# A hybrid layer on one core: the last small product of a triangular inverse takes a turning bank, and the last attention head is scaled behind the split of the memory keys

## The chip, the cores and the metric

The kernel runs on one core of a Trainium2 chip. The time is that of one execution on the device in microseconds (us); less is better. The engines named below are TensorE (PE in the profile; PEld is its loading of weights), VectorE (DVE), ScalarE (ACT), GpSimd (POOL) and SyncE (SP, which issues most of the transfers). PSUM is the memory into which TensorE writes; the kernel uses it in eight banks of 128 partitions by 512 fp32 numbers.

## The reference, cut to what matters

One inference step of one layer for 512 prompt tokens and 64 sample tokens, D = 1024, all in fp32:

```python
h = x + concat(GDN(n), DiffAttn(n)) @ w_out          # n = rmsnorm(x), one projection n @ w_in feeds both
h = h + MemCrossAttn(rmsnorm(h), mk, mv)             # mk, mv = rmsnorm(mem) @ w_mem_k, @ w_mem_v
h = h + relu(rmsnorm(h) @ w_ff1) ** 2 @ w_ff2
y = rmsnorm(h)
```

Two pieces of it are touched. The gated delta group (GDN, 4 heads of 128) goes over the tokens in chunks; in each chunk it solves a unit lower triangular system and carries a state:

```python
a_sys = where(strict, b[:, None] * kk * gam, 0) + eye(C)      # kk = k k^T, gam = decay between tokens
u = triangular_solve(a_sys, b * v);  w = triangular_solve(a_sys, b * exp(G) * k)
vn = u - w @ S
o  = qg @ S + qk @ vn
S  = S * exp(G_last) + kd.T @ vn                              # kd = k * exp(G_last - G): the state product
```

The differential attention (4 heads of 128) ends each head with a norm over its 128 numbers: `ob = rmsnorm(ob, diff_norm) * (1 - lam_init)`, and the heads go through `w_out`. The keys and values of the memory (256 tokens) are projections of their own.

## The kernel before

Activations lie with the features on the partitions. A projection takes 128 columns of a weight at a time: the weight block is loaded (512 KB), ACT casts its high part (`wh`, L159), DVE subtracts it for the low part (`wl`, L160, 128x1024), and 40 matmuls (8 of 512 columns, 8 of 256, 24 of 320) sum high and low parts in a bank of the tag `pr`, which turns over three banks. All matmuls are recorded at L106/107 (`mm`), all transposes at L111/113 (`tr`), so tiles tell them apart.

The eight PSUM banks are dealt by tag: `pr` 3, `ba` 2, `g0`, `g1` and `gs` one each. The banks of a tag turn in the order in which the program asks for them: the third user of `ba` waits until the first user's readers are done. The same holds for the SBUF tiles with two buffers, `kd` among them. A scheduler lays down one fixed order of instructions for each engine, by due times and by these dependencies; on the chip each engine runs its list strictly from the top, so an instruction that waits holds up whatever stands behind it on that engine.

**GDN.** The prompt is cut into chunks 0 to 3 of 128 tokens; the sample's 64 tokens are chunk 4, with half as many products. Each chunk has a preparation and a scan. `gdn_prep` (L653) works on the bank `g0` or `g1` by the chunk's parity. It turns the keys (`each(tr, kb)`) and makes `kd` of them (L680, DVE) and their squares (L682 ACT, L683 DVE); turns the queries (L686, L687); makes the decay, `At` = the strict part of the system (L712), `KQ` (L716) and `vb` (L719). Then it inverts the triangular system by doubling: X = I - B and its transpose (L736, L737, L752, L753), and levels of block size 2, 4, 8, 16, 32 (the loop from L757). A level is two transposes and a small product on one bank, a copy of the one (ACT, L765) and a masked copy of the other (DVE, L766), a second product, and two subtractions (DVE, L773 and L774; the last level has only L774). After the last level four transposes give X (ACT copy L776). In chunks 0 to 3 the two halves of 64 are then joined: a small product `by` (from `At` and `Dt`, 64x64 for each head, L779 to L781), its copy (ACT, L782), a second small product with X (on g0/g1), and L786 writes the last block of X.

`gdn_scan` (L814) carries the state: products on the bank `gs` give `r` (L830), `vn` (L833) and the output, and the state product kd x vn, four products of 128x128, goes to a bank of the tag `ba` (L841); four DVE operations (L797) add it to S. The program asks for the work in the order: preparation of chunk 0; then for c = 0 to 3 the preparation of chunk c+1, and behind it the scan of chunk c. Within c = 0 there stand also `turn_memory` (L905), which turns the normed memory tokens over the `ba` banks, and the projection of z. The projections of the attention heads fill the gaps on TensorE.

**Attention heads.** `diff_project(h)` projects q, k and v of head h and turns k and v over `ba`; head 0's k is written to memory that the normed memory tokens of `turn_memory` held. `diff_head(h, between)` does the head: scores, softmax, values, and the sum of squares `so`. `factors()` (POOL, L1118 and L206) makes the norm's factors `co` from it. `finish()` (L1124) scales the head (`an` = `an` * `co`, DVE 128x640, L1127), turns it over `ba` and writes it for `w_out` with ACT (L1133). A head's `finish` runs within the next head, the last one's within the memory projections, where also the split of the turned memory keys stands (`split_turned`, DVE, L1154).

The names in rows of the order end in numbers: `g0_310`, `g1_328`, `ba_319` are the 310th, 328th and 319th tile asked for (a second number is the program's own).

Of the kernel before, what the change touches and what calls it, by code (L numbers as in the profile page):

```python
# [11 lines left out]
ALU = mybir.AluOpType  # L12
# [3 lines left out]
P = 128  # L16
# [8 lines left out]
H = 4  # L25
# [12 lines left out]
def hybrid_layer_kernel(  # L38
# [9 lines left out]
    nc = tc.nc  # L48
    V, A, G = nc.vector, nc.scalar, nc.gpsimd
# [29 lines left out]
    def nm(s):  # L79
        uid[0] += 1  # L80
        return f"{s}_{uid[0]}"

    def pair(slot, dt=F32):

        return up.tile([P, 2, 4, T], dt, tag=f"u{slot}", name=nm("u"))
# [6 lines left out]
    def small(tag, shape, bufs=None, dt=F32):  # L92
        tag = SHARED.get(tag, tag)
        bufs = 1 if tag in ("vn", "on", "S", "qz") or tag[:-1] in ("At", "Dt", "Y") else 2
        return sp.tile(shape, dt, tag=tag, name=nm(tag), bufs=bufs)

    def tiny(shape, tag="tiny", bufs=16):
        return tp.tile(shape, F32, tag=tag, name=nm(tag), bufs=bufs)

    def bank(tag="ba"):  # L100
        return ps.tile([P, 512], F32, tag=tag, name=nm(tag), bufs=BANKS[tag])
# [4 lines left out]
    def mm(out, lhsT, rhs, start=True, stop=True, pin=False, skip_group_check=False):  # L106
        i = nc.tensor.matmul(out, lhsT, rhs, start=start, stop=stop, skip_group_check=skip_group_check)  # L107
        if pin:
            tc.keep_in_program_order(i)

    def tr(out, in_, pin=False):  # L111
        n = in_.shape[0]
        i = nc.tensor.transpose(out, in_, ident[:n, :n])  # L113
        if pin:
            tc.keep_in_program_order(i)
# [37 lines left out]
    def split_weights(w, shape):  # L153
        raw = wp.tile(shape, F32, tag="raw", name=nm("raw"), bufs=3)
        nc.sync.dma_start(raw, w.rearrange("(k p) n -> p k n", p=P))
        wh = wp.tile(shape, F32R, tag="wh", name=nm("wh"))
        wl = wp.tile(shape, F32R, tag="wl", name=nm("wl"))
        with tc.high_priority():
            A.copy(wh, raw)  # L159
            V.tensor_tensor(wl, raw, wh.bitcast(F32), ALU.subtract)  # L160
        return wh, wl
# [43 lines left out]
    def rpow(out, in_, n=None):  # L205
        G.tensor_tensor(out, in_, bc(nhalf[: in_.shape[0], 0:1], list(in_.shape)), ALU.pow)  # L206
# [419 lines left out]
    def v4(ap, nb):  # L626
        return ap.rearrange("p (h n) -> p h n", h=4)[:, :nb, :]
# [25 lines left out]
    def gdn_prep(c, nb, L):  # L653
# [91 lines left out]
        def pairs(b, half, f):  # L745
            t = b[:, 256 * half : 256 * half + np_ * P].rearrange("p (i n) -> p i n", n=P)
            for i in range(np_):
                f(t[:, i, :], i)
            return t
# [7 lines left out]
        while lv <= last:  # L757
# [6 lines left out]
            by = pairs(b, 0, lambda o, i: mm(o, As[:, i, :], low[:, i * n : (i + 1) * n]))  # L764
# [11 lines left out]
        A.copy(X, each(tr, of(Dt)))  # L776
        if lv < size:
            G.memset(Y[:64, :, :64], 0.0)
            by = bank(f"g{c % 2}")  # L779
            for h in range(H):  # L780
                mm(by[64:, h * 64 : h * 64 + 64], At[:, h, 64:], Dt[:, h, :64])  # L781
            A.copy(Y[64:, :, :64], by[64:, :256].rearrange("p (h n) -> p h n", h=4))  # L782
            bx = bank(f"g{c % 2}")
            for h in range(H):
                mm(bx[:64, h * 64 : h * 64 + 64], Y[:, h, :64], X[:, h, 64:])
            V.tensor_scalar(  # L786
                X[:64, :, 64:], bx[:64, :256].rearrange("p (h n) -> p h n", h=4), -1.0, None, ALU.mult
            )
# [125 lines left out]
    S, behind = None, lambda: None  # L914
    prepared = [gdn_prep(*chunks[0])]
    for c, _, L in chunks[:4]:
# [5 lines left out]
        S, behind = gdn_scan(c, L, prepared[c], S)  # L922
# [152 lines left out]
    def diff_head(h, between):  # L1075


        hs = slice(h * P, (h + 1) * P)
        so, co = tiny([P, 5], "ta"), tiny([P, 5], "ta")
        on = small("an", [P, 5, P])  # L1080
        for t in (4, 0, 1, 2, 3):
            if t == 1:
                between()
            q0 = QT[t][0]
            nk = q0 + P if t < 4 else PAST + DEC
            nb = (nk + P - 1) // P
            if t == 4:
                sample_rows(h, hs, so, on)
                continue
            pr = {}  # L1090
            mx, l = tiny([P, 2], "ta"), tiny([P, 2], "ta")
            for c in (1, 0):
                b = bank(f"g{c}")
                for j in range(2):
                    mm(b[:, :nk], qs[h % 2][:, c, q0 : q0 + P], stacked[h][c][j][:, :nk], start=j == 0, stop=j == 1)
                V.memset(b[:64, nk - 64 : nk], -1e30)
                V.tensor_reduce(mx[:, c : c + 1], b[:, :nk], AX.X, ALU.max)
                V.tensor_scalar(mx[:, c : c + 1], mx[:, c : c + 1], -0.125, None, ALU.mult)
                p = small(f"p{c}", [P, 512])
                A.activation(p[:, :nk], b[:, :nk], AF.Exp, bias=mx[:, c : c + 1], scale=0.125, accum_out=l[:, c : c + 1])  # L1100
                pr[c] = p
            V.reciprocal(l, l)
            V.tensor_tensor(l[:, 1:2], l[:, 1:2], nlam, ALU.mult)
            V.tensor_scalar(pr[1][:, :nk], pr[1][:, :nk], l[:, 1:2], None, ALU.mult)
            V.scalar_tensor_tensor(pr[0][:, :nk], pr[0][:, :nk], l[:, 0:1], pr[1][:, :nk], ALU.mult, ALU.add)
            bt = bank()
            aT = small("aT", [P, 4, P])
            for kb in range(nb):
                tr(bt[:, kb * P : (kb + 1) * P], pr[0][:, kb * P : (kb + 1) * P])
            A.copy(aT[:, :nb, :], v4(bt, nb))  # L1110
            po = bank("gs")[:, :P]
            for kb in range(nb):
                mm(po, aT[:, kb, :], vtm[:, kb, hs], start=kb == 0, stop=kb == nb - 1)
            A.activation(pr[1][:, :P], po, AF.Square, accum_out=so[:, t : t + 1])
            A.copy(on[:, t, :], po)

        def factors():
            G.tensor_scalar(so, so, 1.0 / P, EPS, ALU.mult, ALU.add)  # L1118
            rpow(co, so)

        if h == H - 1:
            factors()

        def finish():  # L1124
            if h < H - 1:
                factors()
            V.tensor_tensor(on, on, co.unsqueeze(2).to_broadcast([P, 5, P]), ALU.mult)  # L1127
            b, b2 = bank(), bank()
            for t in range(4):
                tr(b[:, t * P : (t + 1) * P], on[:, t, :])  # L1130
            tr(b2[:, :P], on[:, 4, :])
            for src, ts_ in ((b, slice(0, SEQ)), (b2[:, DEC:P], slice(SEQ, T))):
                A.activation(od[:, h, ts_], src, AF.Identity, scale=dn)  # L1133

        return finish

    finish = lambda: None
    for h in range(H):
# [4 lines left out]
        finish = diff_head(h, finish)  # L1143
# [30 lines left out]
    for w, out in ((w_mem_k, o_mk), (w_mem_v, o_mv)):  # L1174
        dst = tokens
        for f in range(2):
            fs = slice(512 * f, 512 * f + 512)
            bs = [bank("pr") for _ in range(2)]
            for kc in range(4):
                wt = split_weights(w[0, 256 * kc : 256 * kc + 256, fs], [P, 2, 512])  # L1180
                if kc == 1:
                    turn_keys()
                    if out is o_mv and f == 0:
                        finish()
                for k in (2 * kc, 2 * kc + 1):
                    for t in range(2):
                        ts_ = slice(t * P, (t + 1) * P)
                        for j, (wi, x) in enumerate(((0, mh), (0, ml), (1, mh))):
                            mm(
                                bs[t], x[:, k, ts_], wt[wi][:, k % 2, :],  # L1190
                                start=(k == 0 and j == 0), stop=(k == KT - 1 and j == 2),
                            )
            for t in range(2):
                (A.copy if t else V.tensor_copy)(dst[:, t, fs], bs[t])
                if out is o_mv:
                    A.copy(mv[:, t, fs], dst[:, t, fs])
                    V.tensor_tensor(mvl[2 * t + f], dst[:, t, fs], mv[:, t, fs].bitcast(F32), ALU.subtract)
            nc.sync.dma_start(out[0, 0].rearrange("(b p) h d -> p b (h d)", p=P)[:, :, fs], dst[:, :, fs])
            turn_keys = key_turns(f, dst) if out is o_mk else lambda: None
            if out is o_mv and f == 0:  # L1200
                ob = pair(5, F32R)
                for h in range(H):
                    split_to((ob,), od[:, h, :], h, 0)
# [513 lines left out]
```

## Time and profile before

| what | value |
|---|---|
| median of 3 runs | 977.6 us (976.36 to 977.66) |
| profiled execution | 977.09 us, of which the span of the profile is 975.3 us |
| TensorE busy | 960.4 us, 98% of the span |
| VectorE / ScalarE / GpSimd busy | 689.4 / 536.9 / 66.6 us |
| HBM | 92 GB/s over the span |
| granted TensorE clock | 0.998 |

A row of the timeline gives the start in the span, the duration, engine, line, operation, tile written <- tiles read, and in square brackets the idle time before it with what ended it. A row of groups by source line gives the least, median and greatest duration in ns and from when to when the line ran. A row of windows gives a stretch of the span, its length, and the busy time (and count) of PE, PEld, DVE, ACT and POOL in it, the granted clock, the share of the DMA engines and GB/s. In rows of the trace the numbers of the tiles are left out, so `g` is a tile of g0 or g1.

### The profile page before, as it was taken

What the parts mean: (1) busy time and instruction counts of PE and PEld (TensorE: products, weight loads), DVE (VectorE), ACT (ScalarE), POOL (GpSimd) and SP (SyncE); (2) the same over time, 40 slices, a digit from 0 to 9 for tenths busy, and PEclk for the clock granted to TensorE, in tenths of its full rate; (3) what the DMA queues carried; (4) which work ended last, traced back from release to release, by engine and by line L of the source; (5) the groups of instructions that cost most, each with busy time, mean ns of one, the idle gap of its engine ahead of it and who ended that gap; (6) DMA issues with size and microseconds to landing.
All of it is one profiled execution on the core that took longest, in us unless ns stands there. A gap on an engine that the chain in (4) does not pass through costs nothing.

```text
span 975.3 us, 16991 instructions
## 1 busy us (share of the span) xinstructions
PE 960.4 (98%) x6399; PEld 889.9 (91%) x6399; DVE 689.4 (71%) x1508; ACT 536.9 (55%) x1218; POOL 66.6 (7%) x158
## 2 busy tenths in 40 slices
PE   9999999998999999999999999999999999999996
PEld 7999998997888878999999999999999999999996
DVE  6655777776867776666657888567867779978674
ACT  6664774533656765435445567665544444545444
POOL 4341020211010000000000000000000000000000
PEclk9999999999999999999999999999999999999999
DMA  7442332120744666341121423332323223322202
GB/s 209 117 138 77 95 125 66 46 64 23 187 122 122 219 182 196 87 130 44 45 65 44 141 69 96 90 88 88 87 81 87 87 87 87 87 87 87 66 23 97
DMA packets 124915, 96.01 MB, mean 98 GB/s; under 512 B 6204, under 2 KB 112846, under 8 KB 124322
## 3 DMA queue, kind: packets, MB, share of 16 engines
q1 hardware_dynamic: 124466, 94.28, 33.6%
q8 instruction: 50, 0.82, 0.4%
q10 hardware_dynamic: 368, 0.66, 0.2%
q14 instruction: 31, 0.25, 0.1%
HBM read 79.93 MB, written 9.75 MB: 92 GB/s over the span
## 4 chain that ended last, share of the span: by engine, by line
PE 58%; issue 2%; DVE 1%; ACT 1%; DMA 0%; POOLq 0%; POOL 0%; ACTq 0%; DVEq 0%; SPq 0%
PE pr L107 37%; PE ba L107 10%; PE g L107 6%; PE gs L107 4%; PE ba L113 1%; DMA raw<-in_w_ff_dram 0%; ACT u L1596 0%; ACT c L1504 0%; DVE u L1552 0%; DVE w2l L1458 0%; ACT c L1503 0%; DVE w L1357 0%; DVE wl L1357 0%; DVE wh L1357 0%; ACT wl L1356 0%
## 5 line engine op out<-in xcount | busy, mean ns | idle before, releaser
L107 PE MATMUL pr<-u,wh 128*128 128x320 f32 (+2 forms) x1240 | 325.9, 341 | 0.1
L107 PE MATMUL pr<-u,wl 128*128 128x256 f32 (+1 forms) x816 | 226.1, 301 | 0.0
L107 PEld LDWEIGHTS pr<-u,wh 128*128 128x128 f32 x1240 | 212.1, 189 | 15.2 <-ACT u L286 0.3
L107 PEld LDWEIGHTS pr<-u,wl 128*128 128x128 f32 x816 | 150.5, 189 | 2.5 <-DVE wl L387 0.2
L160 DVE TENSOR_TENSOR wl<-raw,wh 128x1024 fp32r<-128x1024 f32 x65 | 79.5, 1223 | 56.5 <-ACT wh L159 56.3
L159 ACT CAST wh<-raw 128x1024 fp32r<-128x1024 f32 x65 | 68.2, 1049 | 61.9 <-PE pr L107 46.6
L107 PE MATMUL pr<-u,w2h 128*128 128x320 f32 (+1 forms) x384 | 98.5, 341 | 0.0
L1457 ACT CAST w2h<-r 128x512 fp32r<-128x512 f32 x56 | 34.7, 620 | 87.6 <-PE pr L107 85.4
L107 PE MATMUL pr<-f,w2h 128*128 128x320 f32 (+1 forms) x288 | 74.5, 341 | 0.5 <-DVE u L1546 0.5
L107 PEld LDWEIGHTS pr<-u,w2h 128*128 128x128 f32 x384 | 65.0, 188 | 4.5 <-ACT u L1542 0.3
L107 PE MATMUL pr<-u,w2l 128*128 128x256 f32 (+1 forms) x256 | 65.2, 296 | 0.0
L1544 DVE TENSOR_TENSOR u<-u,pr 128x256 f32<-128x256 f32 x96 | 42.4, 450 | 17.1 <-PE pr L107 16.5
L206 POOL TENSOR_TENSOR tiny<-tiny,nhalf 128x1 f32<-128x1 f32 (+4 forms) x10 | 8.8, 879 | 651.3 <-DVE tiny L1610 514.1
L107 PE MATMUL ba<-u,wl 128*128 128x288 f32 x360 | 52.9, 296 | 0.0
L107 PEld LDWEIGHTS pr<-f,w2h 128*128 128x128 f32 x288 | 48.8, 188 | 4.5 <-issue 1.7
L107 PEld LDWEIGHTS ba<-u,wl 128*128 128x128 f32 x360 | 49.2, 188 | 0.6 <-ACT keep L1494 0.5
L107 PE MATMUL pr<-f,w2l 128*128 128x256 f32 (+1 forms) x192 | 48.9, 295 | 0.0
L107 PEld LDWEIGHTS pr<-u,w2l 128*128 128x128 f32 x256 | 47.0, 189 | 1.5
L1458 DVE TENSOR_TENSOR w2l<-r,w2h 128x512 fp32r<-128x512 f32 x56 | 38.5, 688 | 9.6 <-ACT w2h L1457 9.4
L107 PE MATMUL pr<-wh,u 128*128 128x512 f32 x128 | 41.6, 400 | 0.1
L1503 ACT ACTIVATE c<-c 128x288 f32<-128x288 f32 x48 | 20.6, 443 | 28.5 <-DVE c L1502 28.5
L107 PEld LDWEIGHTS pr<-f,w2l 128*128 128x128 f32 x192 | 35.2, 189 | 1.1
(552 smaller groups left out, 2024.8 us busy)
## 6 DMA issues: line engine op xcount, KB each, us to landing
raw<-in_w_ff_dram SPq DMA_DIRECT2D x36, 512.0 KB
raw<-in_w_in_dram SPq DMA_DIRECT2D x28, 512.0 KB
r<-in_w_ff_dram SPq DMA_DIRECT2D x56, 256.0 KB
raw<-in_w_mem_k_dram SPq DMA_DIRECT2D x8, 512.0 KB
raw<-in_w_mem_v_dram SPq DMA_DIRECT2D x8, 512.0 KB
raw<-in_w_out_dram SPq DMA_DIRECT2D x8, 512.0 KB
raw<-in_w_mem_q_dram SPq DMA_DIRECT2D x8, 512.0 KB
raw<-in_w_mem_o_dram SPq DMA_DIRECT2D x8, 512.0 KB
```

Source lines behind the costliest of these rows:

```text
L107: i = nc.tensor.matmul(out, lhsT, rhs, start=start, stop=stop, skip_group_check=skip_group_check)
L113: i = nc.tensor.transpose(out, in_, ident[:n, :n])
L159: A.copy(wh, raw)
L160: V.tensor_tensor(wl, raw, wh.bitcast(F32), ALU.subtract)
L206: G.tensor_tensor(out, in_, bc(nhalf[: in_.shape[0], 0:1], list(in_.shape)), ALU.pow)
L1457: A.copy(wh, src)
L1458: V.tensor_tensor(wl, src, wh.bitcast(F32), ALU.subtract)
L1503: A.activation(c, c, AF.Relu)
L1544: V.tensor_tensor(am, am, b, ALU.add)
```

## The change

Three edits:

1. In `gdn_prep` the last step's small product `by` takes a bank of the turning tag `ba` where it took the chunk's own bank g0/g1 (chunks 0 to 3).
2. `factors()` is called at the end of each head. Before, only the last head did that; the others called it at the beginning of `finish`.
3. The last head's `finish` is handed the last instruction recorded so far, which belongs to the split of the memory keys, and its scaling is held behind that instruction.

```diff
@@ gdn_prep
         if lv < size:
             G.memset(Y[:64, :, :64], 0.0)
-            by = bank(f"g{c % 2}")
+            by = bank()
             for h in range(H):
                 mm(by[64:, h * 64 : h * 64 + 64], At[:, h, 64:], Dt[:, h, :64])
             A.copy(Y[64:, :, :64], by[64:, :256].rearrange("p (h n) -> p h n", h=4))
@@ diff_head
-        if h == H - 1:
-            factors()
-
-        def finish():
-            if h < H - 1:
-                factors()
-            V.tensor_tensor(on, on, co.unsqueeze(2).to_broadcast([P, 5, P]), ALU.mult)
+        factors()
+
+        def finish(behind=None):
+            with tc.issue_after(behind) if behind is not None else ExitStack():
+                V.tensor_tensor(on, on, co.unsqueeze(2).to_broadcast([P, 5, P]), ALU.mult)
             b, b2 = bank(), bank()
@@ the memory projections
                     if out is o_mv and f == 0:
-                        finish()
+                        finish(nc.cur_bb.bb.instructions[-1])
```

The order of instructions that the scheduler lays down differs well beyond these lines. Three places follow.

**TensorE, from the state product of chunk 1's scan to the preparations of chunks 3 and 4.** `ba_319` is that state product, `g0_310` the last transposes of chunk 2's inverse and `g0_311` or `ba_311` the small product that is edited; `g1_328` is the second set of transposes of chunk 3's preparation; `g1_361`, `g1_362`/`ba_362` are the same of chunk 3's inverse, `ba_370` the state product of chunk 2's scan, and `g0_379` is the second set of transposes of chunk 4's preparation. Before:

```order
L107 MATMUL ba_319_2101<-vn_317_2090,kd_196_1456 128x128
L107 MATMUL pr_527_3020<-u_6_91,wh_525_3016 128x512
...
L107 MATMUL g0_303_2018<-Y0_291_1967,X_290_1966 128x128 x2
L113 MATMUL g1_328_2131<-ident_79,u_4_78 128x128 x4
...
L113 MATMUL g0_310_2052<-ident_79,Dt0_292_1968 128x128 x4
...
L113 MATMUL g0_379_2346<-ident_79,u_4_78 128x128 x2
...
L113 MATMUL g1_361_2269<-ident_79,Dt1_343_2185 128x128 x4
```

and now:

```order
L113 MATMUL g0_310_2052<-ident_79,Dt0_292_1968 128x128 x4
L107 MATMUL ba_311_2059<-Dt0_292_1968,At0_283_1941 64x64 x4
L107 MATMUL ba_319_2101<-vn_317_2090,kd_196_1456 128x128 x4
...
L113 MATMUL g1_328_2131<-ident_79,u_4_78 128x128 x4
...
L113 MATMUL g1_361_2269<-ident_79,Dt1_343_2185 128x128 x4
L107 MATMUL ba_362_2276<-Dt1_343_2185,At1_335_2160 64x64 x4
L107 MATMUL ba_370_2318<-vn_368_2307,kd_274_1907 128x128 x4
L107 MATMUL g1_363_2282<-X_341_2183,Y1_342_2184 64x64 x4
L113 MATMUL g0_379_2346<-ident_79,u_4_78 128x128 x2
L107 MATMUL g0_384_2362<-triu2_1096,gg2_1184 128x128 x2
```

The state product of chunk 1 stood in the second level of chunk 2's inverse and now stands behind the whole of it; the preparation of chunk 3, which began before chunk 2's last levels, now begins after them, and that of chunk 4, which began amid chunk 3's levels, after those. Between `g1_328` and the first matmul of head 2's projection (`pr_605`) there stood 66 matmuls of the tag `pr` and now stand none: all 66 come ahead of `g1_328`, and with them 10 transposes, 8 products of 128x128 and 8 of 64x64 more than before.

**TensorE, the turning of the memory tokens.** `ba_233` is the small product of chunk 1, `ba_237` the first of `turn_memory`, `pr_457` a projection whose bank is that of `pr_445`, head 0's k. Before, `ba_237` stood 130 rows further up, in the preparation of chunk 0; now:

```order
L107 MATMUL g1_231_1597<-Y1_213_1516,X_212_1515 128x128 x2
L107 MATMUL pr_454_2699<-u_7_92,wl_453_2696 128x256
L107 MATMUL pr_454_2699<-u_7_92,wh_452_2695 128x512
L113 MATMUL g1_232_1601<-ident_79,Dt1_214_1517 128x128 x4
L107 MATMUL ba_233_1608<-Dt1_214_1517,At1_205_1490 64x64 x4
L113 MATMUL ba_237_1626<-ident_79,u_4_78 128x128 x4
L107 MATMUL pr_457_2723<-u_6_91,wh_452_2695 128x320 x2
```

What moved is the turning of the memory tokens: it follows the small product, and the evacuation of `pr_445` into the memory of those tokens follows it.

**VectorE, the scaling of the last head.** `an_706` is the head, `ta_705` its factors, `At0`, `At1`, `Dt0`, `Dt1` the low parts of the turned memory keys. Before:

```order
L160 TENSOR_TENSOR wl_791_4280<-raw_789_4277,wh_790_4279 128x1024
L1154 TENSOR_TENSOR At0_754_4122<-ba_784_4233,u_753_4121 128x512
L1127 TENSOR_TENSOR an_706_3948<-an_706_3948,ta_705_3947 128x640
L200 TENSOR_TENSOR u_810_4403<-u_2_76,u_810_4403 128x576
L1154 TENSOR_TENSOR At1_755_4123<-ba_785_4240,u_753_4121 128x512
L160 TENSOR_TENSOR wl_796_4303<-raw_794_4300,wh_795_4302 128x1024
```

and now (the lines of this part are two lower in the changed kernel, L1152 for L1154 and L1125 for L1127):

```order
L1152 TENSOR_TENSOR At0_754_4122<-ba_784_4233,u_753_4121 128x512
L200 TENSOR_TENSOR u_810_4403<-u_2_76,u_810_4403 128x576
L1152 TENSOR_TENSOR At1_755_4123<-ba_785_4240,u_753_4121 128x512
L1152 TENSOR_TENSOR Dt0_756_4124<-ba_800_4324,u_753_4121 128x512
L160 TENSOR_TENSOR wl_809_4381<-raw_807_4378,wh_808_4380 128x1024
L1152 TENSOR_TENSOR Dt1_757_4125<-ba_801_4331,u_753_4121 128x512
L1125 TENSOR_TENSOR an_706_3950<-an_706_3950,ta_705_3949 128x640
```

The scaling stands behind all four splits of keys, and the split of the weights `wl_796`, which stood behind it, has gone ahead to a place above this piece.

## The prediction

> **What bounds the kernel now.** I read the page first: the span, the busy shares and the chain of work that ended last.
>
> ```profile
> span 975.3 us, 16991 instructions
> PE 960.4 (98%) x6399; PEld 889.9 (91%) x6399; DVE 689.4 (71%) x1508; ACT 536.9 (55%) x1218; POOL 66.6 (7%) x158
> PE 58%; issue 2%; DVE 1%; ACT 1%; DMA 0%; POOLq 0%; POOL 0%; ACTq 0%; DVEq 0%; SPq 0%
> ```
>
> TensorE is busy for 98% of the span, and every other engine has a small share of the chain. Only 14.9 us (975.3 - 960.4) of TensorE's span are empty, so the kernel gets faster by at most that much unless work is removed, and this change removes none. It can get slower by any amount, if the order leaves TensorE without work. So the question is what the new order does to the stretch in which a chain of other engines runs beside the projections. That is the stretch of the last two inverses, from chunk 3's second transposes to head 2's projection:
>
> ```profile
> 199.37 0.60 PE L113 MATMUL g<-ident,u 128*128 128x128 f32 x4
> 232.49 0.66 PE L113 MATMUL g<-ident,Dt 128*128 128x128 f32 x4
> 245.96 0.48 PE L107 MATMUL pr<-u,wh 128*128 128x512 f32 x1
> ```
>
> These are `g1_328`, `g1_361` and `pr_605` of the order. The windows view of all engines has this stretch in its first row; the next two are of the tag `pr` alone, there and in the plain projections by `w_out`:
>
> ```profile
> 199.37:245.96 46.59, 43.94 (x348) 39.53 (x347) 34.15 (x91) 19.09 (x55) 7.74 (x18) 1.00 0.13 35
> 199.37:245.96 46.59, 15.09 (x66) 10.01 (x67) 1.48 (x4) 0.74 (x2) 1.00 0.13 35
> 400.00:425.00 25.00, 25.00 (x160) 23.58 (x159) 5.23 (x12) 0.00 (x0) 1.00 0.30 85
> ```
>
> Before, TensorE is empty there for only 2.65 us of 46.59, because 66 projection matmuls fill the gaps of the chain. The last row prices them: 25.00 us for 160 matmuls, 0.156 us each (busy times of short runs, as the 15.09, overlap and are too high).
>
> **Edit 1, the work that moves.** The banks of `ba` turn in the program's order, and there the preparation of chunk c+1 stands ahead of the scan of chunk c. So the new small product takes its bank ahead of that scan's state product, and the state product cannot start before the inverse has ended. Behind it hangs `kd` of chunk c+2: two buffers, of which the state product reads the older. TensorE's order shows all of it: state product behind the inverse, next preparation behind the state product. Preparations that overlapped now follow each other, and the fillers are used up ahead of them.
>
> Ahead of `g1_328` come 66 matmuls of `pr`, 66 x 0.156 = 10.3 us, and 10 transposes, 8 products of 128x128 and 8 of 64x64. Each product is two pieces. A piece of 128 costs (0.83 - 0.39) / 4 = 0.11 us by the state product's rows:
>
> ```profile
> 194.34 0.83 PE L107 MATMUL ba<-vn,kd 128*128 128x128 f32 x6
> 195.57 0.39 PE L107 MATMUL ba<-vn,kd 128*128 128x128 f32 x2
> ```
>
> That is 1.1 us for the transposes (at the same price), 1.8 us for 16 pieces, and 0.9 us for 16 pieces of half the width. Together **14.1 us** later for `g1_328`. None of it is new work. It is lost exactly if the stretch from `g1_328` to `pr_605` does not become 14.1 us shorter without it.
>
> **Edit 1, the length of the stretch.** Its chain, worked out from rows. One full level and the last step of chunk 3, in the timeline, and one line of groups:
>
> ```profile
> 229.43 0.41 PE L113 MATMUL g<-ident,Y 128*128 128x128 f32 x2
> 230.38 0.37 ACT L765 COPY X<-g 128x256 f32<-128x256 f32 x1 [3.02 <-PE g L107]
> 230.78 0.42 DVE L766 SCALAR_TENSOR_TENSOR Y<-lev,g 128x256 f32<-128x256 f32 x1 [0.31 <-ACT X L765]
> 231.26 0.71 PE L107 MATMUL g<-Y,X 128*128 128x128 f32 x4
> 232.01 0.42 DVE L774 TENSOR_TENSOR Dt<-Dt,g 128x256 f32<-128x256 f32 x1
> 233.33 0.58 ACT L776 COPY X<-g 128x512 f32<-128x512 f32 x1
> 233.96 0.68 PE L107 MATMUL g<-Dt,At 128*64 128x64 f32 x8 [0.60 <-ACT X L776]
> 234.68 0.37 ACT L782 COPY Y<-g 64x256 f32<-64x256 f32 x1 [0.49 <-PE g L107]
> 235.19 0.65 PE L107 MATMUL g<-X,Y 128*64 128x64 f32 x8 [0.55 <-ACT Y L782]
> 235.87 0.42 DVE L786 TENSOR_SCALAR X<-g 64x256 f32<-64x256 f32 x1 [0.99 <-PE g L107]
> L773 DVE TENSOR_TENSOR Y<-Dt,g x20: 220/284/294, 145.9 to 246.1; 128x128 f32<-128x128 f32 x16, 128x64 f32<-128x64 f32 x4
> ```
>
> Each row here starts when the one above it has ended: nothing in a level can run beside the chain but other work. A last level is 232.49 - 229.43 = 3.06 us; the other four add L773, 0.28. Five levels: 5 x 3.06 + 4 x 0.28 = **16.4 us**. The last step takes 235.87 + 0.42 - 232.49 = 3.8 us, of which the small product's 0.68 now runs beside the copy: 3.1 us.
>
> The head of a preparation is bound by VectorE. Prices by groups:
>
> ```profile
> L680 DVE TENSOR_TENSOR kd<-g,kdc x5: 417/680/691, 117.4 to 221.1; 128x512 f32<-128x512 f32 x4, 128x256 f32<-128x256 f32 x1
> L683 DVE TENSOR_REDUCE tg<-B x5: 419/672/686, 126.7 to 222.7; 128x4 f32<-128x512 f32 x4, 128x2 f32<-128x256 f32 x1
> L712 DVE SCALAR_TENSOR_TENSOR At<-g,tg,Y x18: 330/340/351, 134.7 to 229.2; 128x128 f32<-128x128 f32 x18
> L833 DVE TENSOR_TENSOR vn<-gs,tg x4: 671/692/692, 169.8 to 237.8; 128x512 f32<-128x512 f32 x4
> L753 DVE COPY Y<-g x5: 284/416/424, 142.1 to 234.6; 128x256 f32<-128x256 f32 x4, 128x128 f32<-128x128 f32 x1
> L160 DVE TENSOR_TENSOR wl<-raw,wh x65: 1204/1225/1227, 29.1 to 561.5; 128x1024 fp32r<-128x1024 f32 x65
> L797 DVE SCALAR_TENSOR_TENSOR S<-S,egl,ba x16: 342/342/348, 196.0 to 283.3; 128x128 f32<-128x128 f32 x16
> ```
>
> Chunk 3's head, from `g1_328` to its first level, holds on VectorE one split of weights (1.2), twelve operations of 128x512 at about 0.685 (8.2; four of them, L812, L851, L830 and L833, are the scan's), four of L712 (1.4), L753 (0.4) and small ones (estimated 0.25): **11.5 us**. Behind the last step (3.1) follow two of L797 and chunk 4's half-size L680: 3.1 + 0.7 + 0.4 = **4.2 us**. Chunk 4's head is half as wide: the scan's four at 0.69 (2.8), eight at 0.42 (3.3), four of 0.34 (1.4), L753 (0.3) and small ones (0.3): **8.1 us**. `pr_605` now stands behind the third level's second product of chunk 4; a half-size level, from its transposes to the next level's:
>
> ```profile
> 239.09 0.27 PE L113 MATMUL g<-ident,Y 128*128 128x128 f32 x1
> 241.54 0.30 PE L113 MATMUL g<-ident,Y 128*128 128x128 f32 x1
> ```
>
> That is 2.45 us, and half of one to the second product: 2.5 x 2.45 = **6.1 us**. The sum is 11.5 + 16.4 + 4.2 + 8.1 + 6.1 = 46.3 us with VectorE never waiting in the heads; I add 2 us, an estimate of one hand-over to TensorE and ScalarE or two in each. So 48.3 us against 46.59 before: the stretch does not get shorter, and is 1.7 us longer. Bounds: if the scans' eight operations and the split of weights cost the chain nothing and nothing waits, 46.3 - 5.6 - 1.2 = 39.5 us, -7.1; at the pace of before, where head and levels of chunk 3 took 232.49 - 199.37 = 33.1 us against my 27.9, it is 53.5 us, +6.9.
>
> The gain that edit 1 can bring is inside this sum: the idle 0.60 us ahead of the row 233.96. [...]
>
> **Edit 1, the memory tokens.** `turn_memory` now follows the small product of chunk 1. `pr_457`, next on TensorE, needs the bank of `pr_445`, head 0's k. That is evacuated into the memory of the tokens, so after `ba_237`, by ScalarE and VectorE:
>
> ```profile
> L192 ACT COPY u<-pr x18: 353/372/379, 106.5 to 641.3; 128x256 f32<-128x256 f32 x18
> L193 DVE TENSOR_TENSOR u<-pr,u x18: 361/419/425, 107.6 to 641.7; 128x256 f32<-128x256 f32 x18
> ```
>
> 0.37 + 0.42 us and about 0.5 us for the transposes' run-out, estimated from 0.60 for four: **1.3 us** idle at the top of TensorE's list, between 0 (if the deposits are late anyway) and 1.6.
>
> **Edits 2 and 3.** The norm's factors on POOL take two small instructions a head and only move earlier; what hides them is the next head, and POOL is busy 7%. Without that cover they cost what the last head's scaling waits now:
>
> ```profile
> 352.88 1.16 POOL L206 TENSOR_TENSOR ta<-ta,nhalf 128x5 f32<-128x5 f32 x1
> 354.08 0.83 DVE L1127 TENSOR_TENSOR an<-an,ta 128x640 f32<-128x640 f32 x1 [1.97 <-POOL ta L206]
> 355.49 0.68 DVE L1154 TENSOR_TENSOR At<-ba,u 128x512 fp32r<-128x512 f32 x1
> 357.36 0.50 PE L107 MATMUL pr<-wl,u 128*128 128x512 f32 x1 [0.71 <-DVE wl L160]
> ```
>
> VectorE stood 1.97 us for the factors, and a split of keys and a split of weights were queued behind; TensorE waited 0.71 us for that split. With the scaling behind all key splits this wait goes: **-0.7 us**. Late next is the scaled head, which `w_out` needs; the rest of the value projection covers it. Bounds: -1.5 (part of the 1.97) to +0.8 (the scaling's 0.83 in front of another split of weights).
>
> **The sum.** 14.1 + 1.7 + 1.3 - 0.7 = +16.4 us on the profiled 977.09 (span 975.3 and 1.8 around it), 993.5 us. The median stands 0.5 us above that execution; I take **993.5 us**, since my hand-over term is no better than that.
>
> **Rivals.**
>
> *The stretch shrinks (chance 0.09).* At the lower bound of 39.5 us, with no wait at the tokens, the sum is 14.1 - 7.1 - 0.7 = +6.3; if TensorE's later empty time (part of the 14.9 us) gives 2 us back, +4: 981 to 984 us. For it: the scan's operations could wait. Against it: VectorE's fixed order has them in the heads, ahead of the operations that the inverse needs.
>
> *Faster: the chain was held up by the fillers (0.04).* Without the 66 matmuls in its way the stretch would take less than 46.6 - 14.1 - 1.3 = 31.2 us, and what counts is the removed waits of 0.6 and 0.71 us: 976 us. It decides once both heads together take under 31.2 - 16.4 - 4.2 - 6.1 = 4.5 us. For it: row 230.38 has ScalarE waiting 3.02 us for TensorE. Against it: VectorE alone needs 39.5 - 26.7 = 12.8 us for the two.
>
> *TensorE's clock falls (0.07).* The stretch would leave TensorE empty for a third or more of the time. Windows of the last step and of the end of the span:
>
> ```profile
> 232.40:246.00 13.60, 11.08 (x89) 9.30 (x89) 8.15 (x24) 7.54 (x24) 1.61 (x4) 1.00 0.23 59
> 950.00:975.00 25.00, 17.43 (x134) 17.17 (x132) 10.25 (x21) 11.14 (x21) 1.55 (x2) 0.91 0.28 94
> ```
>
> At 81% busy in gaps of a microsecond the clock stayed 1.00; at 70% it was 0.91. At 0.91 the stretch's 30 us of TensorE work (43.94 - 14.1) take 3 us more; with a clock of half speed for a third of them, 10 us: 997 to 1004 us. Against it: each gap of the new chain is one ScalarE or VectorE operation or two, under 2 us. [...]
>
> *Forecast (0.80): 985 to 1001 us.* That edit 1 does nothing for the inverse itself is inside it: the second small product needs both copies, and if they come one after the other as before, 0.7 us more.
>
> **How the numbers follow.** A change under 0.2% (2 us) cannot be told from none here. Faster: the second rival, 0.04. Same: 0.03, cut from the first rival's lower tail. Slower: 0.93. The range, 983 to 1002 us, takes in both bounds of the stretch (+6.3 and +23) and the nearer parts of the first and third rival.
>
> **What would show it.** Right: a TensorE row `g<-ident,u` about 14 us later than 199.37 + 1.3, no `pr` rows from there to head 2's projection, VectorE and ScalarE named as releasers of most of TensorE's idle time there, and a stretch of 45 to 52 us. The wait of `pr` for the split near 357 us gone. Wrong: `pr` rows inside the stretch, a stretch of 32 us, or a clock under 0.95 in it.

## The result, and the profile after

The changed kernel takes 1005.1 us (median of 4 runs, 1004.86 to 1007.35) against 977.6 us before (4 runs beside it): the ratio is 1.0287, 95% interval 1.0272 to 1.0302. It is 27.5 us slower. The forecast was 993.5 us with a range of 983 to 1002: the direction was right, the size was not, and the time lies 3 us above the range.

The page of the changed kernel: the span, the busy times, and the granted clock in 40 slices (each digit tenths of full speed).

```profile
span 1003.3 us, 17001 instructions
PE 973.6 (97%) x6399; PEld 896.9 (89%) x6399; DVE 693.1 (69%) x1508; ACT 538.4 (54%) x1218; POOL 67.0 (7%) x158
PEclk9999999996899999999999999999999999999999
```

TensorE's busy time rose by 13.2 us with the same 6399 matmuls. By my estimate a part of this is that matmuls in short runs count for more (the 66 of `pr` in the stretch counted 15.09 us before, 0.229 us each, against 0.156 in full runs); for the rest matmuls themselves became longer (the four transposes of chunk 3's last step 1.12 us, against 0.66). The two digits 6 and 8 in the row of the clock, at about 225 to 275 us, say where. The windows view has the stretch, before and now:

```profile
225.00:250.00 25.00, 22.38 (x168) 19.39 (x167) 18.05 (x52) 12.28 (x37) 3.50 (x9) 1.00 0.27 74
225.00:250.00 25.00, 17.41 (x95) 14.41 (x96) 7.88 (x19) 6.41 (x17) 1.93 (x5) 0.69 0.00 0
```

Of 25 us TensorE is now busy 17.4 at a clock of 0.69, and no transfer runs. The next rows are the timeline's: what lies ahead of chunk 3's second transposes (216.14), the starts of its five levels and of its last step (227.03 to 246.79), chunk 4's second transposes (253.79) and first level (264.15), and head 2's projection (271.30).

```profile
214.42 1.04 ACT L159 CAST wh<-raw 128x1024 fp32r<-128x1024 f32 x1 [2.86 <-PE pr L107]
215.49 0.60 ACT L682 ACTIVATE B<-g 128x512 f32<-128x512 f32 x1
216.14 0.66 PE L113 MATMUL g<-ident,u 128*128 128x128 f32 x4 [1.76 <-ACT B L682]
227.03 0.44 PE L113 MATMUL g<-ident,Y 128*128 128x128 f32 x2
230.49 0.41 PE L113 MATMUL g<-ident,Y 128*128 128x128 f32 x2
233.96 0.41 PE L113 MATMUL g<-ident,Y 128*128 128x128 f32 x2 [0.93 <-DVE Dt L774]
237.94 0.66 PE L113 MATMUL g<-ident,Y 128*128 128x128 f32 x2 [0.93 <-DVE Dt L774]
242.57 0.66 PE L113 MATMUL g<-ident,Y 128*128 128x128 f32 x2 [0.93 <-DVE Dt L774]
246.79 1.12 PE L113 MATMUL g<-ident,Dt 128*128 128x128 f32 x4 [0.52 <-DVE Dt L774]
253.79 0.44 PE L113 MATMUL g<-ident,u 128*128 128x128 f32 x2 [1.84 <-ACT B L682]
264.15 0.33 PE L113 MATMUL g<-ident,Y 128*128 128x128 f32 x1
271.30 0.50 PE L107 MATMUL pr<-u,wh 128*128 128x512 f32 x1
```

There is no `pr` row between 216.14 and 271.30, as the order said. This locates the loss of 28.0 us of span (1003.3 - 975.3) in three pieces:

| piece | before | after | difference | forecast |
|---|---|---|---|---|
| chunk 3's second transposes start | 199.37 | 216.14 | +16.8 | +15.4 (14.1 and 1.3) |
| from there to head 2's projection | 46.6 | 55.2 | +8.6 | +1.7 |
| the rest, to the end | | | +2.7 | -0.7 |

The levels show the clock at work. The first two, at a clock of 1.00, take 3.46 and 3.47 us, near the 3.34 of the working; then, with the clock at 0.50 from 234.68 us on, 3.98, 4.63 and 4.22 (the last without L773). The four transposes that took 0.66 before take 1.12. The longest of TensorE's waits in this stretch are short, and all are for ScalarE and VectorE (us in total, times, longest):

```profile
PE g L107 <- DVE Y L766: 3.9, 4, 1.0
PE g L113 <- ACT B L682: 3.6, 2, 1.8
PE g L113 <- DVE Dt L774: 3.3, 4, 0.9
PE g L113 <- DVE X L737: 1.8, 1, 1.8
```

What edit 1 was to do, it does: the small product starts beside ScalarE's copy, which took its place ahead of it before (chunk 2's last step, timeline):

```profile
210.42 0.68 PE L107 MATMUL ba<-Dt,At 128*64 128x64 f32 x8
210.58 0.59 ACT L776 COPY X<-g 128x512 f32<-128x512 f32 x1 [2.48 <-PE g L113]
211.19 0.37 ACT L782 COPY Y<-ba 64x256 f32<-64x256 f32 x1
212.12 0.68 PE L107 MATMUL g<-X,Y 128*64 128x64 f32 x8
```

### The profile page after: what moved, and what is told of

It reads as the page before. It is cut to its first block, busy times and chain, and to the rows that moved or that the text cites. A ratio compares the mean times of both kernels' runs of the same rounds, so it can differ in the third digit from the quotient of the medians.

```text
span 1003.3 us, 17001 instructions
## 1 busy us (share of the span) xinstructions
PE 973.6 (97%) x6399; PEld 896.9 (89%) x6399; DVE 693.1 (69%) x1508; ACT 538.4 (54%) x1218; POOL 67.0 (7%) x158
## 4 chain that ended last, share of the span: by engine, by line
PE 87%; DVE 5%; ACT 3%; issue 2%; DMA 1%; POOL 1%; POOLq 0%; SPq 0%; ACTq 0%; DVEq 0%
PE pr L107 54%; PE g L107 11%; PE ba L107 11%; PE gs L107 6%; PE ba L113 2%; PE g L113 2%; ACT wh L159 0%; DVE p L459 0%; DMA raw<-in_w_ff_dram 0%; DMA u<-in_x_prompt_dram 0%; ACT u L221 0%; POOL tiny L206 0%; DVE u L231 0%; DVE an L1125 0%; POOL ta L206 0%
## 5 line engine op out<-in xcount | busy, mean ns | idle before, releaser
L1542 DVE TENSOR_TENSOR u<-u,pr 128x256 f32<-128x256 f32 x96 | 42.3, 448 | 17.4 <-PE pr L107 16.8
```

The source lines that it names most:

```text
L1542: V.tensor_tensor(am, am, b, ALU.add)
```

## The experiments

The theory after the result: the state product, late by its turn in `ba`, holds back the next preparation through `kd`; the chain that is left half empties TensorE, and its clock falls. Rivals: a part of the loss is in edits 2 and 3; the late state product itself, not `kd`, holds up the scans; the clock is only a sign and costs nothing.

All ratios are to runs of the kernel before on the same chip; the intervals are of 95%. Differences in us are between medians.

| run | median, us | ratio to before |
|---|---|---|
| bank_alone | 1004.6 | 1.0277 (1.0263 to 1.0291) |
| finish_alone | 981.0 | 1.0035 (1.0021 to 1.0048) |
| kd_three | 977.2 | 0.9993 (0.9985 to 1.0002) |
| fill | 1002.4 | 1.0254 (1.0240 to 1.0268) |
| bank_c01 | 981.9 | 1.0048 (1.0034 to 1.0062) |
| bank_c2 | 992.2 | 1.0146 (1.0129 to 1.0163) |
| bank_c3 | 988.7 | 1.0110 (1.0094 to 1.0125) |
| factors_alone | 981.9 | 1.0046 (1.0032 to 1.0060) |
| scale_alone | 976.5 | 0.9990 (0.9981 to 0.9999) |
| kd_alone | 979.3 | 1.0028 (1.0017 to 1.0040) |
| kd_bank | 975.3 | 0.9978 (0.9969 to 0.9987) |
| kd_bank_scale | 974.5 | 0.9968 (0.9955 to 0.9980) |

### Which edit: bank_alone and finish_alone

bank_alone is the kernel before with edit 1 only; finish_alone is the changed kernel with the bank put back:

```diff
-            by = bank()
+            by = bank(f"g{c % 2}")
```

> Edit 1 without edits 2 and 3. Theory (the turn of the banks puts the state product behind the inverse, and the next preparation behind the state product): the whole loss is here, 1005 us within 2 us, with chunk 3's second transposes (g<-ident,u x4) near 216 us and the first matmul of head 2's projection near 271 us, as in the changed kernel. Rival (the later scaling of the last head or the earlier factors make a part of the loss): under 1000 us.

> Edits 2 and 3 without edit 1. Theory: about 0.7 us less than before, 976.9 us (976 to 978), the wait of TensorE for the split of weights near 357 us gone (0.71 us before), no other move. Rival (these edits carry part of the loss, or bring a wait in w_out): over 980 us.

Edit 1 alone costs 26.9 us, with chunk 3's second transposes at 216.08 and head 2's projection at 272.45 us: nearly the whole loss is its own. Edits 2 and 3 alone cost 3.3 us where 0.7 less were expected. This part of the forecast had the wrong sign (two runs below). The two do not add up: on top of edit 1 they cost 0.5 us, which is within the spread of the runs.

### Is kd the link: kd_three

The changed kernel, with chunk 2's `kd` in a buffer of the heads' `aT` tiles, which have the same shape and are used later. The small product keeps its turn ahead of the state product.

```diff
-        kd = sb("kd")[:, :nb]
+        kd = sb("aT" if c == 2 else "kd")[:, :nb]
```

> All three edits, but chunk 2's kd lies in a buffer of its own (that of the heads' aT tiles), so that the preparations of chunks 3 and 4 no longer wait for the state product just before them. The small product still takes its turn in ba ahead of the state product. Theory (kd is the link by which the late state product holds back the next preparation): nearly all of the loss goes, 976 to 984 us, projection matmuls stand between the levels of chunk 3 again, and the clock stays at 1.00 in 200 to 275 us. Rival (the state product behind the inverse holds up the scans themselves, or the bank's turn costs by itself): 990 us or more.

977.2 us: one buffer takes 28 us back. The windows view over 200 to 275 us, of the changed kernel and then of this one:

```profile
200.00:275.00 75.00, 59.08 (x361) 50.14 (x360) 40.91 (x101) 23.03 (x61) 8.41 (x19) 0.82 0.13 34
```

```profile
200.00:275.00 75.00, 73.56 (x533) 65.91 (x533) 54.12 (x155) 36.80 (x112) 6.04 (x15) 1.00 0.40 103
```

TensorE gets 172 more matmuls done in the same 75 us, and its clock stays at 1.00. The state product still stands behind the inverse in TensorE's order here (chunk 1's at 209.37 us, behind the small product at 208.76), so its lateness costs the scans nothing that shows. The rival that it holds up the scans falls.

### What the clock costs: fill

The changed kernel with work added that nothing reads, on the other chunk's bank: two products in each level of chunk 3 and four in chunk 4's head.

```diff
+        fill = bank("g0") if c == 3 else None
         while lv <= last:
...
             A.copy(Xs, bt)
+            if fill is not None:
+                mm(fill[:, :256], Xs[:, 0, :], At[:, :2, :].rearrange("p h n -> p (h n)"))
...
+            if fill is not None:
+                mm(fill, Yc[:, 0, :], At.rearrange("p h n -> p (h n)"))
```

> All three edits, and work added that nothing reads: in chunk 3's inverse each level has one more product of 256 and one of 512 columns on the other chunk's bank, beside the copies of ScalarE and VectorE, and chunk 4's head has four of 512 columns, some 14 more matmuls, about 10 us of TensorE at full clock. Theory (the half-empty chain lets the granted clock fall to 0.5, and that lengthens the products in the chain itself): the clock stays at 1.00, a level of chunk 3 takes 3.4 to 3.5 us throughout where it took 4.0 to 4.6 us, and the time falls by 3 to 7 us to 998 to 1002 us although work was added. Rival (the low clock costs nothing since ScalarE and VectorE set the pace): the time stays or rises, 1004 to 1012 us.

The time falls by 2.7 us to 1002.4 although 14 products (28 matmuls in the trace) were added; 3 to 7 us were expected. In its timeline the starts of chunk 3's five levels and of its last step, chunk 4's second transposes and first level, and head 2's projection, and the window of the levels:

```profile
226.80 0.44 PE L113 MATMUL g<-ident,Y 128*128 128x128 f32 x2
230.25 0.41 PE L113 MATMUL g<-ident,Y 128*128 128x128 f32 x2
233.72 0.41 PE L113 MATMUL g<-ident,Y 128*128 128x128 f32 x2
237.36 0.41 PE L113 MATMUL g<-ident,Y 128*128 128x128 f32 x2 [0.24 <-DVE Dt L789]
240.83 0.41 PE L113 MATMUL g<-ident,Y 128*128 128x128 f32 x2
244.06 0.60 PE L113 MATMUL g<-ident,Dt 128*128 128x128 f32 x4
249.36 0.38 PE L113 MATMUL g<-ident,u 128*128 128x128 f32 x2
258.81 0.33 PE L113 MATMUL g<-ident,Y 128*128 128x128 f32 x1
267.13 0.49 PE L107 MATMUL pr<-u,wh 128*128 128x512 f32 x1
```

```profile
227.00:247.00 20.00, 18.37 (x115) 13.30 (x114) 6.99 (x18) 5.43 (x15) 1.94 (x5) 1.00 0.00 1
```

The levels take 3.45, 3.47, 3.64, 3.47 and 3.23 us at a clock of 1.00, and the stretch from chunk 3's second transposes (215.91 here) to head 2's projection is 51.2 us in place of 55.2. By the windows the clock here has a mean of 0.93 in 200 to 225 us, as in the changed kernel, and is 1.00 in 225 to 275. In the changed kernel it is at 0.50 from 217.62 to 221.03 us, in chunk 3's head, and eight matmuls there take 1.98 us (217.48); here they take 1.94 (217.25), and nothing was added at that place. So the low clock behind that head costs some 3.9 us of the stretch or more, unless the added work shortens it in another way, which nothing shows; 1.4 us come back behind the stretch (733.4 us from head 2's projection to the end against 732.0). The rival that the clock costs nothing falls. The larger part of the loss stays without it.

### Chunk by chunk: bank_c01, bank_c2, bank_c3

The kernel before, with the turning bank in some chunks only, as here in chunk 2:

```diff
-            by = bank(f"g{c % 2}")
+            by = bank("ba" if c == 2 else f"g{c % 2}")
```

> Edit 1 in chunks 0 and 1 only. The order keeps state products 1 and 2 and the preparations of chunks 3 and 4 where they were; the turning of the memory tokens moves behind chunk 1's inverse. Theory: within 2 us of before, 976 to 980 us, and the 1.3 us that were forecast for the wait at the memory tokens do not show. Rival (every chunk costs alike): 990 us.

> Edit 1 in chunk 2 only. State product 1 stands behind chunk 2's inverse and chunk 3's preparation behind that; chunk 4's preparation lies amid chunk 3's last levels still. Theory: a part of the loss, 983 to 993 us, and TensorE's clock falls below 1.00 for a shorter time or not at all. Rival (one late chunk is absorbed by the projections that are left): under 980 us.

> Edit 1 in chunk 3 only. State product 2 stands behind chunk 3's inverse and chunk 4's preparation behind that; chunk 3's preparation overlaps chunk 2's inverse as before. Theory: a part of the loss, 980 to 990 us; with chunk 2's part it adds up to less than the whole 27 us, since the low clock (about 4 us) needs both. Rival: under 979 us.

Chunks 2 and 3, whose product delays the state product that chunk 3's and chunk 4's `kd` wait for, cost 14.8 and 11.3 us, chunks 0 and 1 together 4.5. The stretch of 225 to 250 us, for chunks 0 and 1, for chunk 2 and for chunk 3:

```profile
225.00:250.00 25.00, 19.11 (x148) 15.98 (x147) 17.71 (x52) 11.54 (x36) 3.56 (x9) 1.00 0.23 60
```

```profile
225.00:250.00 25.00, 20.31 (x131) 17.49 (x129) 15.39 (x45) 9.19 (x28) 3.58 (x9) 0.85 0.00 1
```

```profile
225.00:250.00 25.00, 19.03 (x101) 15.72 (x101) 12.40 (x32) 5.64 (x14) 1.94 (x5) 0.73 0.08 22
```

Two expectations missed. Chunks 0 and 1 were to cost nothing: in this stretch TensorE is busy 19.11 us against 22.38 before, so work that filled it was done earlier. I read this as chunk 2's preparation waiting for the state product of chunk 0 in the same way. The timelines agree (that state product starts at 175.62 us against 172.02 before, chunk 2's `kd` at 176.89 against 174.19), but no run took it apart. And the low clock does not need both late chunks: with chunk 2 alone its mean is 0.94 in 200 to 225 us, 0.85 in 225 to 250 and 1.00 in 250 to 275, with chunk 3 alone 1.00, 0.73 and 1.00, and in the changed kernel 0.93, 0.69 and 0.83. Chunks 2 and 3 add up to 26.1 us, hardly less than the whole 26.9, where I expected some 4 us less. With chunks 0 and 1 the parts make 30.5 us, so they are not independent.

### Edits 2 and 3: factors_alone and scale_alone

The kernel before with one of the two edits each, as in the diff of the change.

> Edit 2 alone: the factors begun behind every head. Both edits together (2 and 3) measured 3.4 us slower than before. Theory: the loss is in this edit; head 0's factors (1.2 us on POOL) now stand ahead of the sample scan's factors, and head 0's scaling (0.8 us on VectorE) ahead of the sample rows' softmax, so that TensorE is empty 2.7 us longer in 275 to 350 us: 980.5 to 982.5 us. Rival (the scaling held behind the key splits costs it): 977 to 978.5 us.

> Edit 3 alone: the last head's scaling held behind the split of the memory keys. Theory: TensorE's wait of 0.71 us for the split of weights near 357 us goes, nothing else moves: 976.3 to 977.3 us. Rival (it is this edit that costs the 3.4 us): 979.5 us or more.

Edit 2 costs 4.5 us, edit 3 gains 1.0. VectorE's timeline around head 0's scaling, in the kernel before:

```profile
278.25 0.85 DVE L881 TENSOR_TENSOR vn<-gs,tg 64x256 f32<-64x256 f32 x2
287.26 0.82 DVE L1127 TENSOR_TENSOR an<-an,ta 128x640 f32<-128x640 f32 x1
```

and with edit 2 alone, with the matmul that waited (the scaling is L1124 there):

```profile
278.86 0.83 DVE L1124 TENSOR_TENSOR an<-an,ta 128x640 f32<-128x640 f32 x1 [4.20 <-POOL ta L206]
279.94 0.84 DVE L881 TENSOR_TENSOR vn<-gs,tg 64x256 f32<-64x256 f32 x2
280.93 0.67 PE L107 MATMUL gs<-S,vb 128*128 128x256 f32 x2 [0.75 <-DVE vn L881]
```

With its factors begun early, the scaling was due early too, and the order of VectorE has it ahead of the sample's `vn` (L881) and its softmax, where it stood 9 us behind. VectorE stands 4.20 us for the factors (before, it stood 2.97 us for ScalarE there), and `vn` is 1.7 us late. It is the same at the next head, where the exponential of the softmax (ScalarE, L1058) needs an operation queued behind the scaling, and TensorE needs the exponential:

```profile
308.63 0.82 DVE L1124 TENSOR_TENSOR an<-an,ta 128x640 f32<-128x640 f32 x1 [4.19 <-POOL ta L206]
312.54 0.44 PE L107 MATMUL g<-Dt,qs 128*128 128x128 f32 x2 [0.81 <-ACT p L1058]
```

Over 275 to 350 us, before and with edit 2 alone, TensorE is busy:

```profile
275.00:350.00 75.00, 74.14 (x458) 64.04 (x457) 52.07 (x164) 49.71 (x160) 5.66 (x12) 1.00 0.54 163
```

```profile
275.00:350.00 75.00, 71.55 (x432) 60.08 (x431) 47.91 (x148) 45.04 (x145) 5.78 (x12) 1.00 0.53 162
```

That is 2.6 us emptier and 26 matmuls fewer. The rest of the 4.5 us was not located. Edit 3 alone does what was forecast for it: in 350 to 375 us TensorE is busy for all but 0.01 us, where 0.81 us were empty (before, and with edit 3 alone):

```profile
350.00:375.00 25.00, 24.19 (x120) 19.60 (x119) 17.47 (x21) 15.60 (x25) 1.36 (x2) 1.00 0.58 171
350.00:375.00 25.00, 24.99 (x126) 20.70 (x126) 17.91 (x21) 16.50 (x26) 1.36 (x2) 1.00 0.59 186
```

### A version that is faster: kd_alone, kd_bank, kd_bank_scale

The kernel before with the buffer for chunk 2's `kd`; that with edit 1; and that with edits 1 and 3.

> The kernel before with chunk 2's kd in a buffer of its own, and none of the three edits. Theory (before, the state products stand early enough, and kd's two buffers hold up little): 976 to 978 us. Rival (kd held back the preparations before as well): 975 us or less.

> Edit 1 with chunk 2's kd in a buffer of its own, without edits 2 and 3. With edits 2 and 3 this measured 977.2 us. Theory (edit 2's 2.7 to 3.4 us lie behind the inverses and add up): 973.5 to 975 us. Rival (the inverses' stretch and the heads' stalls cover each other): 976.5 to 978 us.

> Edit 1 with chunk 2's kd in a buffer of its own, and edit 3, without edit 2. Theory: as without edit 3 less 0.7 us, 972.8 to 974.3 us, the fastest of all. Rival: no less than without edit 3.

The buffer by itself costs 1.9 us; with it, edit 1 gains 2.2 us on the kernel before (about 4 us on kd_alone). With edit 3 as well it is 974.5 us, 0.32% less than before (0.20 to 0.45%); the last 0.75 us, between kd_bank and kd_bank_scale, are not clear of the runs' spread. That is the lowest median of all runs here, and shows that the turning bank is worth something once the buffer lets the preparations go. All three times lie above what was expected, kd_alone by 1.3 us, the other two by 0.2 to 0.3. The buffer alone leaves TensorE 1.3 us emptier in 200 to 275 us (70.98 us busy against 72.28); why was not taken further.

## Why the prediction was wrong

**Right: the mechanism of edit 1.** The order of the banks, the state product behind the inverse, `kd` as the link and the fillers used up ahead were named, and kd_three confirms the link: the loss goes with one buffer. That the small product would run beside the copy was in the sum as 0.68 us of the last step, and no row of the kernel before shows it; in the changed kernel it starts 0.16 us ahead of the copy in the same step (247.84 and 248.00), where it stood 0.60 us for it in the row 233.96. The moved work, 14.1 us by the prices of 0.156 and 0.11 us, is found again: chunk 3's second transposes start 16.8 us later. The 2.7 us between are mostly a row that the sum left out there: TensorE waited 1.76 us for L682, which itself stood behind a cast of weights of 1.04 us (214.42). I had priced L680 and what follows for chunk 4, not for chunk 3.

**Failed: the length of the stretch, the step "48.3 us against 46.59".** It measured 55.2, above its own upper bound of 53.5. Term by term, from the rows shown (us; in fill the clock is low in chunk 3's head only):

| term | sum | changed kernel | fill |
|---|---|---|---|
| chunk 3's head | 11.5 | 10.9 | 10.9 |
| its five levels | 16.4 | 19.8 | 17.3 |
| last step, to chunk 4's second transposes | 4.2 | 7.0 | 5.3 |
| chunk 4's head | 8.1 | 10.4 | 9.4 |
| to head 2's projection | 6.1 | 7.1 | 8.3 |
| added for hand-overs | 2.0 | | |
| together | 48.3 | 55.2 | 51.2 |

The clock was taken at 1.00; by fill its fall costs some 3.9 us or more. A full level at a clock of 1.00 held, 3.46 us against 3.34. What else was short lies mostly behind the levels, where the sum counted VectorE's work and had no rows for the way from the end of one operation to the next that needs it: hand-overs there and the added work together make 51.2 - 46.3 = 4.9 us in fill, where I had added 2; these runs do not part them. One missing piece can be named. The state product stands between the two small products in TensorE's order, and the sum had it cost nothing. At a clock of 1.00 the second small product (212.12) starts 0.56 us behind the copy it needs (211.19 + 0.37), where it was 0.14 before (235.19 behind 234.68 + 0.37). In chunk 3's last step, at a clock of 0.50, it starts 1.5 us behind (250.89 behind 249.36).

**Failed: the third rival's chance and price.** It had 0.07 and 997 to 1004 us, and it is what happened on top of the forecast. The row of 70% busy, with the clock at 0.91, is no sign of it as I read it: there TensorE's last matmul ends at 967.43 us, and the clock is 1.00 up to 970 us and 0.50 from 971 on, with no matmul left. The half speed in its price is what came: 0.50 for 27.3 us of the stretch. What I let decide against it was the length of the gaps, under 2 us. They are (the longest wait in the stretch is 1.84 us), and the clock fell all the same: over the stretch it was 0.75, under the 0.95 that the prediction named as a sign of being wrong. That gaps under 2 us leave the clock at 1.00 was my estimate, and the stretch shows the opposite.

**Failed: the wait at the memory tokens, +1.3 us.** In the changed kernel the first matmuls of `pr_457` and the evacuation of `pr_445` stand in these rows:

```profile
171.26 0.55 PE L107 MATMUL pr<-u,wh 128*128 128x320 f32 x2
171.32 0.37 ACT L192 COPY u<-pr 128x256 f32<-128x256 f32 x1 [0.34 <-PE ba L113]
171.73 0.42 DVE L193 TENSOR_TENSOR u<-pr,u 128x256 f32<-128x256 f32 x1 [1.20 <-ACT u L192]
```

The evacuation did wait for the tokens, but TensorE went on without a wait: the matmuls start while `pr_445` is still being read. My claim that they share a bank does not fit these rows.

**Failed in sign: edit 2.** "what hides them is the next head" looked at POOL's two instructions alone. Their cost is not on POOL; it is that the scaling, which follows them, moved on VectorE ahead of the sample's chain. The order of VectorE has it (in the timeline of factors_alone some fifteen rows that stood ahead of head 0's scaling stand behind it), and I had looked only at the place of the last head. Edit 2 costs 4.5 us alone. In the changed kernel VectorE stands 4.25 us for factors too, but the sample's chain comes later there against the heads: `vn` starts at 306.03 us against 305.96 in bank_alone, and edits 2 and 3 together cost 0.5 us.

**Right: edit 3.** Forecast -0.7 us; measured -1.0 us (ratio 0.9990, 0.9981 to 0.9999), with the wait near 357 us gone. And the rival that the kernel would be faster, which needed both heads together under 4.5 us, was rightly put low: they took 10.9 and 10.4 us.

## What to carry to other kernels

A tile that takes its turn in a shared set of buffers is ordered against everything else that turns there: before moving a tile to such a set, list who asks for it next in the program, and what that one's readers release (here: product, state product, `kd`, next preparation). When fillers are used up ahead of a serial chain, count the chain also at the lower clock that TensorE may get in it (here 0.75 over the stretch, with TensorE busy for 40.99 of 55.16 us), and give every hand-over in it a row. Work that is begun earlier also becomes due earlier, so look on the engines of its followers, not on its own.

## What the runs showed of the hardware

TensorE's granted clock fell to half although TensorE was never empty for 2 us in a row: its longest empty time in the stretch of the inverses is the 1.84 us ahead of 253.79 us. The changed kernel has the clock at 0.50 there three times: from 217.62 us for 3.41 us, from 234.68 for 17.07, from 255.16 for 6.83. The windows view has the second of these and, for all three, the 3.41 us just ahead:

```profile
214.20:217.61 3.41, 0.97 (x7) 0.55 (x6) 2.21 (x4) 2.42 (x4) 0.00 (x0) 1.00 0.00 0
231.27:234.68 3.41, 1.51 (x11) 1.22 (x10) 1.66 (x4) 0.92 (x4) 1.62 (x4) 1.00 0.00 0
234.68:251.75 17.07, 11.78 (x54) 9.57 (x52) 3.71 (x10) 2.73 (x8) 0.30 (x1) 0.50 0.00 0
251.75:255.16 3.41, 1.09 (x9) 0.72 (x7) 2.16 (x7) 0.77 (x2) 0.00 (x0) 1.00 0.00 0
```

TensorE is busy for 28%, 44% and 32% of the three rows at 1.00. The longest gap alone does not tell where the matmuls become longer: in the timeline of bank_alone TensorE is empty for 1.54 us ahead of 226.58, and the next products of a level still take 0.62 us for four:

```profile
226.58 0.63 PE L113 MATMUL g<-ident,X 128*128 128x128 f32 x4 [1.54 <-DVE X L737]
228.62 0.62 PE L107 MATMUL g<-Dt,B 128*128 128x128 f32 x4
```

Two levels later the same products take 1.06 us, with no gap over 0.97 us between:

```profile
233.62 0.71 PE L107 MATMUL g<-Y,X 128*128 128x128 f32 x4 [0.97 <-DVE Y L766]
235.26 0.66 PE L113 MATMUL g<-ident,Y 128*128 128x128 f32 x2 [0.93 <-DVE Dt L774]
235.72 1.06 PE L107 MATMUL g<-Dt,B 128*128 128x128 f32 x4
```

These runs do not show why the clock falls where it does. They show what work that nothing reads did to it: in 227 to 247 us fill has TensorE busy for 18.37 of 20 us at a clock of 1.00, the changed kernel for 12.74 us at 0.69, and fill is 2.7 us faster.
